# Weight splits ahead of the other work in an expert stage, with four split and eleven raw buffers

## The chip, the cores and the metric

The kernel runs on one core of a Trainium2 chip. The metric is the device time of one execution in microseconds (us), and the median of several executions is compared. The engines of the core are TensorE (PE: matmuls and transposes), VectorE (DVE), ScalarE (ACT), GpSimd (POOL: here gathers, scatters and three subtractions) and SyncE (SP: it issues the weight fetches). Every engine works through its own instructions strictly in order.

## The reference, cut to what matters

One layer: a token mixer (a long convolution beside a gated recurrence), then a mixture of experts in which each expert chooses its tokens. Everything is float32, D is 1024, there are 1024 tokens and 16 experts, and each expert takes its 128 best tokens. The change touches the experts alone:

```python
gates, idx = lax.top_k(jnp.swapaxes(aff, 1, 2), cap)      # cap = 128 tokens for each of 16 experts
xg = jax.vmap(lambda hb, ib: hb[ib])(h, idx)
a = jnp.einsum('becd,edf->becf', xg, w1)                  # 1024 -> 2048
b = jnp.einsum('becd,edf->becf', xg, w3)
y = jnp.einsum('becf,efd->becd', jax.nn.silu(a) * b, w2)  # 2048 -> 1024
y = y * gates[..., None].astype(y.dtype)
# zeros((N, D)).at[idx].add(y), then x + g2 * that, then a last rmsnorm
```

The three weight arrays hold 16 x 3 x 1024 x 2048 float32 numbers, 402 MB, and each is read once.

## The kernel before

Up to about 1010 us the kernel computes the mixer and the routing. Then the expert stage runs to about 2150 us, and a short tail writes the result.

**Pieces.** The weights come in 384 pieces (NP) of 128 x 2048 float32, 1 MB each, 24 to an expert. `fetch(n)` (L988 to L1005) issues piece n on SP into a `raw` buffer; there are NA + NB = 8 + 5 = 13 of these, in two pools. TensorE multiplies in a rounded float32, so `split(n)` makes two parts of a piece: ScalarE casts it (`ehi`, L1219), VectorE subtracts the cast from the piece (`elo`, L1225; GpSimd does it for the first three, L1223). There are NHI = 3 buffers of each part. `mm3` (L63 to L66) adds three products, hi with hi (L64), hi of the tokens with lo of the weights (L65) and lo with hi (L66); a piece takes 12 matmuls of 512 columns. A cast can begin once TensorE has finished the piece three before; a raw buffer is free once the subtraction has read it, and then SP can issue the fetch of the piece 13 further on.

**Steps.** The loop over i at L1265 has 33 steps; steps 2e and 2e + 1 are the halves of expert e's 2048 columns (fc is 0, then 1). A step takes four pieces of w1 (PSUM banks `pa`), a silu by ScalarE (`sa`, two instructions, L1282), four pieces of w3, a multiplication by VectorE (two, L1284), and then four pieces of w2 for the step before (banks `pb`). `take()` (L1245) is called once for a piece: it makes the split of the piece NHI - 1 further on, issues a fetch, and hands out the parts.

**Other work between the pieces.** After each step eight transposes flip `sa` (L1318), ScalarE casts them (`hh`, two, L1320) and VectorE subtracts (two, L1321). After step 2e come the one-hot matrix of expert e + 2's tokens (VectorE, `oh`, L1184), 16 small matmuls that make their row numbers (L1188), a cast (`idx`, L1190) and an indirect gather on GpSimd (L1193); then `transposed(e + 1)`: eight transposes of that expert's tokens (L1203), eight scaled copies by ScalarE (`hf`, L1209), two casts (`hcT`, L1210) and two subtractions by VectorE (L1211). After step 2e + 2 VectorE scales the result of expert e (two, `xg`, L1307) and GpSimd adds its rows to `xacc` in memory (L1312). Below, the pieces of an expert are numbered 0 to 23 by n modulo 24: its first step's w1 is piece 20 to 23 of the expert before, its w3 is 0 to 3, the next step's w1 is 8 to 11 and its w3 12 to 15, and the w2 pieces are 4 to 7 and 16 to 19.

**What sets the order.** The program is written without waits. A scheduler puts the instructions of each engine into one fixed list when the kernel is built, by its own estimate of when each would be ready and by the order in which they were written; the waits follow from the buffers. `after(ins)` (L1024) asks that what is issued inside it stands behind `ins`.

At the start of the stage three pieces are split (their casts run early, at 985 us, beside the routing), two gathers are issued, nine matmuls of the identity with itself are run with no use of the result (L1261), and the first expert's tokens are transposed.

Of the kernel before, what the change touches and what calls it, by code (L numbers as in the profile page):

```python
# [11 lines left out]
F32 = mybir.dt.float32  # L12
# [10 lines left out]
P = 128  # L23
# [4 lines left out]
NE = 16  # L28
# [29 lines left out]
def kernel(ctx: ExitStack, tc: tile.TileContext, T: dict, out: bass.AP, dbg=None, stop=None):  # L58
# [919 lines left out]
    NA, NB, NHI = 8, 5, 3  # L978
# [200 lines left out]
    found = [None]  # L1179

    def gather(e):

        oh = ep.tile([P, 8, P], BF16, name="oh", bufs=1)
        V.tensor_tensor(oh, iot[:].unsqueeze(1).broadcast_to([P, 8, P]), posT[:, :, e:e + 1].broadcast_to([P, 8, P]), ALU.is_equal)  # L1184
        pi = bank("pt", 2)
# [4 lines left out]
        f_ = V.tensor_copy(idx, pi[:, 0:1])  # L1190
        found[0] = found[0] or f_
        xg = ep.tile([P, D + NE], F32, name="xg", bufs=3)
        G.indirect_dma_start(xg[:], None, h2d[:], bass.IndirectOffsetOnAxis(ap=idx[:, 0:1], axis=0))  # L1193
        return idx, xg

    def transposed(e, xg):
        xT = [a[:, :, e % 2 * P:(e % 2 + 1) * P] for a in hcT]
        for b in range(2):
            pt = bank("pt", 2)
            hf = ep.tile([P, 4, P], F32, name="hf", bufs=2)  # L1200
            for c in range(4):
                k = 4 * b + c
                PE.transpose(pt[:, c * P:(c + 1) * P], xg[:, k * P:(k + 1) * P], ident)  # L1203
            for c in range(4):
                k = 4 * b + c
                if e == 0 and b == 1:
                    V.tensor_scalar(hf[:, c, :], pt[:, c * P:(c + 1) * P], gs2[:, k:k + 1], mod2[:, k, 0:1], ALU.mult, ALU.add)
                else:
                    S.activation(hf[:, c, :], pt[:, c * P:(c + 1) * P], AF.Identity, scale=gs2[:, k:k + 1], bias=mod2[:, k, 0:1])  # L1209
            S.copy(xT[0][:, 4 * b:4 * b + 4, :], hf)  # L1210
            V.tensor_tensor(xT[1][:, 4 * b:4 * b + 4, :], hf, f32(xT[0][:, 4 * b:4 * b + 4, :]), ALU.subtract)  # L1211
        return xT

    def split(n):
        if n < NP:
            raw = raws.pop(n)
            hi = eb.tile([P, 2048], F32R, name="ehi", bufs=NHI)
            with after(tl[7]["row"]):
                S.copy(hi, raw)  # L1219
            lo = eb.tile([P, 2048], F32R, name="elo", bufs=NHI)  # L1220
            if n < NHI:
                with after(pieces[-1]):
                    pieces.append(G.tensor_tensor(lo, raw, f32(hi[:]), ALU.subtract))  # L1223
            else:
                V.tensor_tensor(lo, raw, f32(hi[:]), ALU.subtract)  # L1225
            parts[n] = [t.rearrange("p (a b) -> p a b", b=1024) for t in (hi, lo)]
# [16 lines left out]
    at = 0  # L1243

    def take():  # L1245
        nonlocal at
        if at > 0:
            split(at + NHI - 1)
            fetch(at + NHI - 1 + NA + NB)
        at += 1  # L1250
        return parts.pop(at - 1)

    for n in range(NHI):
        split(n)
        fetch(n + NA + NB)
    g = {0: gather(0)}
    g[1] = gather(1)
# [4 lines left out]
    xTs = {0: transposed(0, g[0][1])}  # L1262
    py = None
    hs_ = {}
    for i in range(NS + 1):  # L1265
# [5 lines left out]
        if i < NS:  # L1271
            sa = ep.tile([P, 2, 512], F32, name="sa")
            for nm in range(2):
                pab = [bank("pa", 4) for _ in range(2)]
                for k in range(8):
                    if k % 2 == 0:
                        w = take()
                    for h in range(2):
                        mm3(pab[h], [a[:, k, :] for a in xTs[e]], [a[:, k % 2, h * 512:(h + 1) * 512] for a in w], k == 0, k == 7)
                for h in range(2):  # L1280
                    if nm == 0:
                        silu = S.activation(sa[:, h, :], pab[h], AF.Silu)  # L1282
                    else:
                        V.tensor_tensor(sa[:, h, :], sa[:, h, :], pab[h], ALU.mult)  # L1284
            if i == NS - 1:
                with after(silu):
                    S.activation(idf, ones[:, 0:1], AF.Abs_reciprocal_sqrt)
        if i > 0:
            pe, pf = divmod(i - 1, 2)
            hh = hs_.pop(i - 1)  # L1290
            if pf == 0:
                py = [bank("pb", 2) for _ in range(2)]
            for c in range(8):
                if c % 2 == 0:
                    w = take()
                for h in range(2):
                    mm3(py[h], [a[:, c, :] for a in hh], [a[:, c % 2, h * 512:(h + 1) * 512] for a in w],
                        pf == 0 and c == 0, pf == 1 and c == 7)
# [4 lines left out]
            if pf == 1:  # L1303
                idx, xg = g.pop(pe)
                for h in range(2):
                    hs = slice(h * 512, (h + 1) * 512)
                    V.scalar_tensor_tensor(xg[:, hs], py[h], xg[:, D + pe:D + pe + 1], g2r[:, hs], ALU.mult, ALU.mult)  # L1307
                    if pe == NE - 1:
                        S.copy(yh[0][:, hs], xg[:, hs])
                        V.tensor_tensor(yh[1][:, hs], xg[:, hs], f32(yh[0][:, hs]), ALU.subtract)  # L1310
                if pe < NE - 1:
                    G.indirect_dma_start(xacc[:], bass.IndirectOffsetOnAxis(ap=idx[:, 0:1], axis=0), xg[:, 0:D], None, compute_op=ALU.add)  # L1312
        if i < NS:
            hh = [ep.tile([P, 8, P], F32R, name=f"hh{i_}") for i_ in range(2)]
            for b in range(2):
                pt = bank("pt", 2)
                for c in range(4):
                    PE.transpose(pt[:, c * P:(c + 1) * P], sa[:, b, c * P:(c + 1) * P], ident)  # L1318
                pv = pt.rearrange("p (c t) -> p c t", t=P)
                S.copy(hh[0][:, 4 * b:4 * b + 4, :], pv)  # L1320
                V.tensor_tensor(hh[1][:, 4 * b:4 * b + 4, :], pv, f32(hh[0][:, 4 * b:4 * b + 4, :]), ALU.subtract)  # L1321
            hs_[i] = hh
            if fc == 0:
                if e + 2 < NE:
                    g[e + 2] = gather(e + 2)
                if e + 1 < NE:
                    xTs[e + 1] = transposed(e + 1, g[e + 1][1])
# [152 lines left out]
```

## Time and profile before

| what | value |
|---|---|
| median of 3 runs | 2182.51 us (2178.77 to 2185.27) |
| the profiled execution's own time | 2179.6 us |
| its span in the trace | 2177.8 us |
| mean granted TensorE clock, as a share of full | 0.982 |
| TensorE matmuls busy | 2042.1 us (94%) |
| VectorE busy | 1732.7 us (80%) |
| ScalarE busy | 1243.4 us (57%) |
| bytes moved | 565.95 MB, mean 260 GB/s |

The shares are means over the whole span. The expert stage is a little over half of it, and the other half works with other limits, so what the change is worth has to be read from rows of the stage itself. Matmuls are pipelined: in the timeline each shows about 0.39 us though the next starts 0.23 us later.

### The profile page before, as it was taken

Reading aid. Unit: us, or ns where it says so; the run is one execution under the profiler, and the core shown is the slowest. Engines: PE = TensorE matmul, PEld = TensorE weight load, DVE = VectorE, ACT = ScalarE, POOL = GpSimd, SP = SyncE. Lnnn points to the kernel's source line nnn. Section 1 sums busy time; section 2 is a strip of 40 time slices with the busy share of each in tenths; the row PEclk is TensorE's granted clock in tenths of the full one; section 3 lists DMA queues with packets and bytes.
Section 4 is the critical chain, followed back from the end, with each engine's and each line's share of the span. In section 5 each row is a group of like instructions: output and inputs, shape, how many; then the busy total and the mean of one; then the engine's idle time right before and its main releaser. Section 6 shows DMA issues by size and latency. Waiting matters only on the chain.

```text
span 2177.8 us, 30396 instructions
## 1 busy us (share of the span) xinstructions
PE 2042.1 (94%) x11761; PEld 1613.6 (74%) x11761; DVE 1732.7 (80%) x2051; ACT 1243.4 (57%) x1463; POOL 204.7 (9%) x241
## 2 busy tenths in 40 slices
PE   7997899899999989994999999999999999999997
PEld 2444788798788867773888888787877878787775
DVE  6678357747878877666999999888988889888887
ACT  3566235444432211242777787777777777777774
POOL 1122100100000011124000000000010011000000
PEclk9999899999999999996999999999999999999999
DMA  7875421320243447376999999999999999999992
GB/s 244 267 261 158 150 73 45 117 83 24 62 137 120 131 141 240 109 256 240 359 375 374 393 392 373 354 377 378 382 361 358 389 381 364 361 381 372 362 335 116
DMA packets 185404, 565.95 MB, mean 260 GB/s; under 512 B 15544, under 2 KB 26379, under 8 KB 185260
## 3 DMA queue, kind: packets, MB, share of 16 engines
q1 hardware_dynamic: 147044, 478.41, 59.1%
q0 software_dynamic: 28784, 76.46, 11.6%
q10 hardware_dynamic: 9432, 9.15, 1.3%
q8 instruction: 93, 1.52, 0.3%
q14 instruction: 51, 0.42, 0.1%
HBM read 522.59 MB, written 41.50 MB: 259 GB/s over the span
## 4 chain that ended last, share of the span: by engine, by line
PE 75%; DVE 9%; DMA 6%; issue 6%; ACT 3%; POOL 1%; DVEq 0%; SPq 0%; ACTq 0%; POOLq 0%
PE pa L65 15%; PE pa L66 15%; PE pa L64 14%; PE pb L66 5%; PE pb L65 5%; PE pb L64 5%; DVE elo L1225 2%; PE pb L849 2%; PE pt L866 2%; PE pf L546 2%; ACT ehi L1219 2%; DMA oraw<-in_w_out 1%; PE pt L1318 1%; DVE arena L731 1%; DVE arena L729 1%
## 5 line engine op out<-in xcount | busy, mean ns | idle before, releaser
L1225 DVE TENSOR_TENSOR elo<-raw,ehi 128x2048 fp32r<-128x2048 f32 x381 | 863.1, 2289 | 102.4 <-ACT ehi L1219 98.3
L1219 ACT CAST ehi<-raw 128x2048 fp32r<-128x2048 f32 x384 | 732.9, 1917 | 214.0 <-PE pb L66 94.6
L65 PE MATMUL pa<-elo,hcT 128*128 128x512 f32 x1024 | 406.8, 397 | 14.9 <-DVE elo L1225 14.6
L66 PE MATMUL pa<-ehi,hcT 128*128 128x512 f32 x1024 | 401.0, 392 | 0.0
L64 PE MATMUL pa<-ehi,hcT 128*128 128x512 f32 x1024 | 376.8, 392 | 2.0 <-ACT hcT L1210 1.4
L65 PEld LDWEIGHTS pa<-elo,hcT 128*128 128x128 f32 x1024 | 192.6, 188 | 72.9 <-DVE elo L1225 35.0
L64 PEld LDWEIGHTS pa<-ehi,hcT 128*128 128x128 f32 x1024 | 192.6, 188 | 42.5 <-ACT hcT L1210 1.8
L66 PEld LDWEIGHTS pa<-ehi,hcT 128*128 128x128 f32 x1024 | 192.8, 188 | 37.3
L65 PE MATMUL pb<-elo,hh 128*128 128x512 f32 x512 | 204.9, 400 | 0.0
L66 PE MATMUL pb<-ehi,hh 128*128 128x512 f32 x512 | 200.0, 391 | 0.4 <-DVE hh L1321 0.4
L64 PE MATMUL pb<-ehi,hh 128*128 128x512 f32 x512 | 184.6, 390 | 0.5 <-ACT hh L1320 0.5
L66 PE MATMUL pa<-hT,wlo 128*128 128x512 f32 x448 | 178.8, 400 | 0.3 <-DVE wlo L580 0.3
L64 PE MATMUL pa<-hT,whi 128*128 128x512 f32 x448 | 178.5, 398 | 0.0
L65 PE MATMUL pa<-hT,whi 128*128 128x512 f32 x448 | 176.4, 394 | 0.0
L1312 POOL DMA_INDIRECT xacc<-xg,idx x15 | 45.3, 3022 | 842.5 <-DVE xg L1307 842.5
L64 PEld LDWEIGHTS pb<-ehi,hh 128*128 128x128 f32 x512 | 96.1, 188 | 21.6 <-ACT hh L1320 0.9
L65 PEld LDWEIGHTS pb<-elo,hh 128*128 128x128 f32 x512 | 96.2, 188 | 21.4
L66 PEld LDWEIGHTS pb<-ehi,hh 128*128 128x128 f32 x512 | 96.2, 188 | 18.8 <-DVE hh L1321 0.9
L66 PEld LDWEIGHTS pa<-hT,wlo 128*128 128x128 f32 x448 | 84.4, 188 | 18.7 <-DVE wlo L580 1.2
L64 PEld LDWEIGHTS pa<-hT,whi 128*128 128x128 f32 x448 | 84.5, 189 | 17.0 <-issue 0.5
L65 PEld LDWEIGHTS pa<-hT,whi 128*128 128x128 f32 x448 | 84.5, 189 | 17.0 <-issue 0.2
L546 PE MATMUL pf<-Yh,mt 128*128 128x256 f32 x256 | 74.5, 424 | 17.6 <-ACT he L552 6.2
(407 smaller groups left out, 3099.3 us busy)
## 6 DMA issues: line engine op xcount, KB each, us to landing
raw<-in_exp_w SPq DMA_DIRECT2D x371, 1024.0 KB, 8.0
aw<-in_ada_w SPq DMA_DIRECT2D x96, 256.0 KB, 4.9
wraw<-in_w_in SPq DMA_DIRECT2D x64, 256.0 KB, 3.3
raw<-in_exp_w POOLq DMA_DIRECT2D x13, 1024.0 KB, 8.7
mt<-in_fwm POOLq DMA_DIRECT2D x64, 128.0 KB, 3.4
Hd<-he ACTq DMA_DIRECT2D x32, 256.0 KB, 3.0
wod<-arena POOLq DMA_DIRECT2D x32, 256.0 KB, 3.4
arena<-in_fwm SPq DMA_DIRECT2D x32, 256.0 KB, 3.9
```

Of the source, the lines that this page charges most:

```text
L64: PE.matmul(ps, lhs[0], rhs[0], start=first, stop=False)
L65: PE.matmul(ps, lhs[0], rhs[1], start=False, stop=False)
L66: PE.matmul(ps, lhs[1], rhs[0], start=False, stop=last)
L546: PE.matmul(pt[:, :HC], mt[:, i, :], Y[:, 2 * n + i, :], start=(i == 0), stop=(i == 1))
L729: V.tensor_tensor(kv, kv, view(F2, h, [[2 * h, nb], [LT - h, 2], [0, h]]), ALU.mult)
L731: V.tensor_tensor(qv, qv, view(F2, LT + h, [[2 * h, nq], [-(LT + h), 2], [0, h]]), ALU.mult)
L849: PE.matmul(px[:, j, :], fm[:, j, i, :], Y[:, 2 * n + i, :], start=(i == 0), stop=(i == 1))
L866: PE.matmul(pz[:, j, :], im[:, i, j, :], pp[:, i, :], start=(i == 0), stop=(i == 1))
L1219: S.copy(hi, raw)
L1225: V.tensor_tensor(lo, raw, f32(hi[:]), ALU.subtract)
L1312: G.indirect_dma_start(xacc[:], bass.IndirectOffsetOnAxis(ap=idx[:, 0:1], axis=0), xg[:, 0:D], None, compute_op=ALU.add)
L1318: PE.transpose(pt[:, c * P:(c + 1) * P], sa[:, b, c * P:(c + 1) * P], ident)
```

## The change

Four things are altered, all in the expert stage.

1. **Buffers**: NB goes from 5 to 3 and NHI from 3 to 4, so there are 11 raw buffers, and 4 for each part. `take` becomes `piece`, which splits the piece three further on instead of two and then runs the jobs that are queued. At the start a fourth piece is split, by VectorE, and a fourth fetch issued.
2. **Order on ScalarE and VectorE**: `act()` and `dve()` put the other work (silu, multiplication, `hh`, `hf`, `hcT`, scale, one-hot) behind the cast or the subtraction of the piece three ahead of the one now handed out.
3. **Jobs**: this work is queued with `then` and issued with the next piece, no longer at the end of a step.
4. **Fixed pieces** for the next experts' work: the one-hot after piece 0 and the gather after piece 2 of an expert's first step, and the token transposes in two halves after pieces 1 and 4 of its second step.

The core of the diff:

```diff
-    NA, NB, NHI = 8, 5, 3
+    NA, NB, NHI = 8, 3, 4
...
+    highs, lows = {}, {}
     def split(n):
...
             with after(tl[7]["row"]):
-                S.copy(hi, raw)
+                highs[n] = S.copy(hi, raw)
...
-            if n < NHI:
+            if n < 3:
                 with after(pieces[-1]):
                     pieces.append(G.tensor_tensor(lo, raw, f32(hi[:]), ALU.subtract))
             else:
-                V.tensor_tensor(lo, raw, f32(hi[:]), ALU.subtract)
+                lows[n] = V.tensor_tensor(lo, raw, f32(hi[:]), ALU.subtract)
...
-    def take():
+    jobs = []
+    def piece():
         nonlocal at
         if at > 0:
             split(at + NHI - 1)
             fetch(at + NHI - 1 + NA + NB)
         at += 1
+        while jobs:
+            jobs.pop(0)()
         return parts.pop(at - 1)
+    def act():
+        return after(highs[min(at + NHI - 2, NP - 1)])
+    def dve():
+        return after(lows[min(at + NHI - 2, NP - 1)])
+    def then(f, *a):
+        jobs.append(lambda: f(*a))
+    def gate(sa, pab, i):
+        for h in range(2):
+            with act():
+                r = S.activation(sa[:, h, :], pab[h], AF.Silu)
...
+    def times(sa, pab):
+        for h in range(2):
+            with dve():
+                V.tensor_tensor(sa[:, h, :], sa[:, h, :], pab[h], ALU.mult)
+    def flip_sa(i, sa):
...
+                PE.transpose(pt[:, c * P:(c + 1) * P], sa[:, b, c * P:(c + 1) * P], ident)
+            with act():
+                S.copy(hh[0][:, 4 * b:4 * b + 4, :], pv)
+            with dve():
+                V.tensor_tensor(hh[1][:, 4 * b:4 * b + 4, :], pv, f32(hh[0][:, 4 * b:4 * b + 4, :]), ALU.subtract)
...
+    def mark(e, ohs):
+        with dve():
+            ohs.append(onehot(e))
-    for n in range(NHI):
+    for n in range(3):
         split(n)
         fetch(n + NA + NB)
-    g = {0: gather(0)}
-    g[1] = gather(1)
+    gather(0, onehot(0))
+    gather(1, onehot(1))
...
-    xTs = {0: transposed(0, g[0][1])}
+    for b in range(2):
+        transposed(0, b)
+    for n in range(3, NHI):
+        split(n)
+        fetch(n + NA + NB)
...
+                    if fc == 0 and e + 2 < NE:
+                        if at_ == 0:
+                            then(mark, e + 2, ohs)
+                        if at_ == 2:
+                            then(lambda e_, o: gather(e_, o[0]), e + 2, ohs)
+                    if fc == 1 and e + 1 < NE and at_ in (1, 4):
+                        then(transposed, e + 1, at_ // 4, act, dve)
+                if nm == 0:
+                    then(gate, sa, pab, i)
+                else:
+                    then(times, sa, pab)
...
+            elif pf == 1:
+                then(add_rows, pe, py)
         if i < NS:
...
+            then(flip_sa, i, sa)
```

The names in the rows below: `ehi` and `elo` are the parts of a piece, `sa` the silu and its product, `hh` the flipped `sa`, `hf` and `hcT` the next expert's tokens; the number behind x is how many such instructions follow each other.

VectorE at the start of the stage, before:

```order
L1170 TENSOR_TENSOR pos_8562<-pb,eq 128x128
L1171 TENSOR_TENSOR posT<-pos_8543,pos_8562 128x128
L1184 TENSOR_TENSOR oh<-iot,posT 128x1024
L1190 CAST idx<-pt 128x1
L1184 TENSOR_TENSOR oh<-iot,posT 128x1024
L1190 CAST idx<-pt 128x1
```

and after the change:

```order
L1170 TENSOR_TENSOR pos_8558<-pb,eq 128x128
L1171 TENSOR_TENSOR posT<-pos_8539,pos_8558 128x128
L1232 TENSOR_TENSOR elo<-raw,ehi 128x2048
L1181 TENSOR_TENSOR oh<-iot,posT 128x1024
L1191 CAST idx<-pt 128x1
L1181 TENSOR_TENSOR oh<-iot,posT 128x1024
```

The subtraction of the fourth piece (L1232) now stands between `posT` and the first one-hot, which was L1184 and is L1181.

ScalarE in expert 5 around a silu, before (from the cast of piece 118 on):

```order
L1219 CAST ehi<-raw 128x2048 x3
L1282 ACTIVATE sa<-pa 128x512
L1219 CAST ehi<-raw 128x2048
L1282 ACTIVATE sa<-pa 128x512
L1219 CAST ehi<-raw 128x2048 x8
```

and after (from the cast of piece 120 on):

```order
L1226 CAST ehi<-raw 128x2048 x4
L1277 ACTIVATE sa<-pa 128x512 x2
L1226 CAST ehi<-raw 128x2048 x8
L1295 CAST hh_11522<-pt 128x512 x2
L1226 CAST ehi<-raw 128x2048 x2
```

The two silu instructions (L1282, now L1277) stood with one cast between them, directly behind the cast of piece 120; now both stand together behind that of piece 123.

ScalarE at the token transposes of expert 6 (pieces 129 to 137, so 9 to 17 of expert 5), before, from the two `hh` casts behind the cast of piece 129 on:

```order
L1320 CAST hh_11488<-pt 128x512 x2
L1219 CAST ehi<-raw 128x2048 x2
L1209 ACTIVATE hf<-pt,mod_79,gs_80 128x128 x5
L1210 CAST hcT_88<-hf 128x4x128
L1209 ACTIVATE hf<-pt,mod_79,gs_80 128x128 x3
L1219 CAST ehi<-raw 128x2048
L1210 CAST hcT_88<-hf 128x4x128
L1219 CAST ehi<-raw 128x2048
L1282 ACTIVATE sa<-pa 128x512 x2
L1219 CAST ehi<-raw 128x2048 x8
```

and after, from the two `hh` casts behind the cast of piece 131 on:

```order
L1295 CAST hh_11522<-pt 128x512 x2
L1226 CAST ehi<-raw 128x2048 x2
L1213 ACTIVATE hf<-pt,mod_79,gs_80 128x128 x4
L1226 CAST ehi<-raw 128x2048
L1215 CAST hcT_88<-hf 128x4x128
L1226 CAST ehi<-raw 128x2048
L1277 ACTIVATE sa<-pa 128x512 x2
L1226 CAST ehi<-raw 128x2048
L1213 ACTIVATE hf<-pt,mod_79,gs_80 128x128 x4
L1226 CAST ehi<-raw 128x2048
L1215 CAST hcT_88<-hf 128x4x128
L1226 CAST ehi<-raw 128x2048 x6
```

All eight scaled copies (L1209, now L1213) stood between the casts of pieces 131 and 132; now four stand in front of the cast of piece 134 and four in front of that of 137, and the silu is between them.

TensorE at the same place, before (piece 129):

```order
L66 MATMUL pa<-ehi,hcT_89 128x512
L64 MATMUL pa<-ehi,hcT_88 128x512
L1203 MATMUL pt<-ident,xg 128x128 x8
L65 MATMUL pa<-elo,hcT_88 128x512
L66 MATMUL pa<-ehi,hcT_89 128x512
```

and after (from the end of piece 131 on):

```order
L65 MATMUL pa<-elo,hcT_88 128x512
L66 MATMUL pa<-ehi,hcT_89 128x512
L1206 MATMUL pt<-ident,xg 128x128 x4
L64 MATMUL pa<-ehi,hcT_88 128x512 x2
L1206 MATMUL pt<-ident,xg 128x128 x4
L65 MATMUL pa<-elo,hcT_88 128x512
```

The eight transposes (L1203, now L1206) stood in piece 129; now they stand at the start of piece 132, with two matmuls between the halves.

## Rows read from the trace of the kernel before

**Rows 1.** The page, part 4: share of the chain by engine.

```profile
PE 75%; DVE 9%; DMA 6%; issue 6%; ACT 3%; POOL 1%; DVEq 0%; SPq 0%; ACTq 0%; POOLq 0%
```

**Rows 2.** The page, part 5: operation | busy us, mean ns | idle, releaser.

```profile
L1225 DVE TENSOR_TENSOR elo<-raw,ehi 128x2048 fp32r<-128x2048 f32 x381 | 863.1, 2289 | 102.4 <-ACT ehi L1219 98.3
L1219 ACT CAST ehi<-raw 128x2048 fp32r<-128x2048 f32 x384 | 732.9, 1917 | 214.0 <-PE pb L66 94.6
```

**Rows 3.** Stretches: us, busy by engine, PEclk, DMA share, GB/s; two whole experts.

```profile
1185.65:1254.27 68.62, 68.62 (x330) 56.72 (x329) 62.67 (x40) 53.41 (x43) 2.71 (x2) 1.00 1.01 384
1462.54:1533.13 70.59, 69.62 (x329) 56.33 (x328) 62.85 (x38) 53.05 (x42) 5.31 (x2) 1.00 1.00 375
1200.00:1250.00 50.00, 50.00 (x226) 41.39 (x225) 45.03 (x26) 36.49 (x22) 0.00 (x0) 1.00 1.01 398
```

**Rows 4.** VectorE timeline, scale of an expert: start, us; 12 more between.

```profile
1185.65 1.41 DVE L1307 SCALAR_TENSOR_TENSOR xg<-pb,xg,g2r 128x512 f32<-128x512 f32 x2
...
2099.94 1.43 DVE L1307 SCALAR_TENSOR_TENSOR xg<-pb,xg,g2r 128x512 f32<-128x512 f32 x2 [0.69 <-PE pb L66]
```

**Rows 5.** Waits of TensorE, 1340 to 2040 us: total, times, longest.

```profile
PE pa L65 <- DVE elo L1225: 9.6, 10, 1.0
```

**Rows 6.** TensorE timeline, last expert: rows with a wait [idle before <-releaser].

```profile
2107.02 0.50 PE L65 MATMUL pa<-elo,hcT 128*128 128x512 f32 x1 [0.38 <-DVE elo L1225]
...
2116.43 0.50 PE L65 MATMUL pa<-elo,hcT 128*128 128x512 f32 x1 [0.96 <-DVE elo L1225]
...
2120.39 0.50 PE L65 MATMUL pa<-elo,hcT 128*128 128x512 f32 x1 [0.90 <-DVE elo L1225]
...
2138.01 0.50 PE L64 MATMUL pb<-ehi,hh 128*128 128x512 f32 x1 [0.45 <-ACT hh L1320]
```

**Rows 7.** Timeline of all engines, one stall of TensorE at 1443 us.

```profile
1433.82 1.91 ACT L1219 CAST ehi<-raw 128x2048 fp32r<-128x2048 f32 x1 [0.81 <-PE pa L66]
...
1438.58 0.60 ACT L1282 ACTIVATE sa<-pa 128x512 f32<-128x512 f32 x1 [2.85 <-PE pa L66]
...
1439.08 1.90 ACT L1219 CAST ehi<-raw 128x2048 fp32r<-128x2048 f32 x1
...
1441.01 4.58 DVE L1225 TENSOR_TENSOR elo<-raw,ehi 128x2048 fp32r<-128x2048 f32 x2 [2.95 <-ACT ehi L1219]
...
1443.35 0.50 PE L65 MATMUL pa<-elo,hcT 128*128 128x512 f32 x1 [0.95 <-DVE elo L1225]
```

**Rows 8.** All waits, 1050 to 2100 us: silu on TensorE.

```profile
ACT sa L1282 <- PE pa L66: 31.5, 12, 2.9
```

**Rows 9.** The page, part 6: fetches of a piece, KB each, us to landing.

```profile
raw<-in_exp_w SPq DMA_DIRECT2D x371, 1024.0 KB, 8.0
```

**Rows 10.** Timeline of all engines, start of the expert stage.

```profile
1008.70 3.96 PE L1261 MATMUL pb<-ident 128*128 128x128 f32 x18
...
1009.54 1.23 DVE L1184 TENSOR_TENSOR oh<-iot,posT 128x1024 bf16<-128x1024 bf16 x1
...
1012.50 0.54 PE L1188 MATMUL pt<-tok,oh 128*128 128x1 bf16 x16
...
1013.53 1.77 POOL L1193 DMA_INDIRECT xg<-h2d,idx  x1 [10.50 <-DVE idx L1190]
...
1018.76 1.97 PE L1203 MATMUL pt<-ident,xg 128*128 128x128 f32 x8 [3.78 <-DMA xg<-h2d,idx]
```

**Rows 11.** The gather line L1193: us to landing.

```profile
DMA to landing us min/median/max: 5.2/8.5/14.1
```

**Rows 12.** Timeline of all engines, flips of the next expert at 1468 us.

```profile
1466.08 1.28 DVE L1321 TENSOR_TENSOR hh<-pt,hh 128x512 fp32r<-128x512 f32 x2
...
1467.99 1.03 PE L1203 MATMUL pt<-ident,xg 128*128 128x128 f32 x8
...
1468.63 1.86 ACT L1209 ACTIVATE hf<-pt,mod,gs 128x128 f32<-128x128 f32 x5 [0.79 <-PE pt L1203]
...
1470.36 0.64 ACT L1210 CAST hcT<-hf 128x512 fp32r<-128x512 f32 x1
```

More of the change, by code (lines that the diff above doesn't have):

```diff
@@ L1177, with onehot, gather @@
     ep = ctx.enter_context(tc.tile_pool(name="ep", bufs=1))
-    found = [None]
-    def gather(e):
+    def onehot(e):
         oh = ep.tile([P, 8, P], BF16, name="oh", bufs=1)
         V.tensor_tensor(oh, iot[:].unsqueeze(1).broadcast_to([P, 8, P]), posT[:, :, e:e + 1].broadcast_to([P, 8, P]), ALU.is_equal)
+        return oh
+    def gather(e, oh):
         pi = bank("pt", 2)
@@ L1261 @@
         PE.matmul(idle[:, 0:P], ident, ident, start=True, stop=True)
-    xTs = {0: transposed(0, g[0][1])}
+    for b in range(2):
+        transposed(0, b)
+    for n in range(3, NHI):
+        split(n)
+        fetch(n + NA + NB)
     py = None
@@ L1272 @@
             sa = ep.tile([P, 2, 512], F32, name="sa")
+            ohs = []
+            xT = tokens_of(e)
             for nm in range(2):
                 pab = [bank("pa", 4) for _ in range(2)]
[L1275 to L1287, printed above, removed]
+                for q in range(4):
+                    w = piece()
+                    for k in (2 * q, 2 * q + 1):
+                        for h in range(2):
+                            mm3(pab[h], [a[:, k, :] for a in xT], [a[:, k % 2, h * 512:(h + 1) * 512] for a in w], k == 0, k == 7)
+                    at_ = 4 * nm + q
+                    if fc == 0 and e + 2 < NE:
[7 more added lines that the diff above has]
+                    then(gate, sa, pab, i)
+                else:
+                    then(times, sa, pab)
         if i > 0:
             pe, pf = divmod(i - 1, 2)
+            while i == NS and jobs:
+                jobs.pop(0)()
             hh = hs_.pop(i - 1)
@@ L1292 @@
                 py = [bank("pb", 2) for _ in range(2)]
[L1293 to L1298, printed above, removed]
+            for q in range(4):
+                w = piece()
+                for c in (2 * q, 2 * q + 1):
+                    for h in range(2):
+                        mm3(py[h], [a[:, c, :] for a in hh], [a[:, c % 2, h * 512:(h + 1) * 512] for a in w],
+                            pf == 0 and c == 0, pf == 1 and c == 7)
             if i == NS:
@@ L1302 @@
                     start_sum(t)
[L1303 to L1312, printed above, removed]
-        if i < NS:
[L1314 to L1327, printed above, removed]
+                add_rows(pe, py)
+            elif pf == 1:
+                then(add_rows, pe, py)
+        if i < NS:
+            then(flip_sa, i, sa)
     for t in range(8):
```

55 lines of the change are left out of this document (38 added, 17 removed).

## The prediction

> **What bounds the kernel now.** I read the chain that ended last first: three quarters of it is TensorE [rows 1]. The costliest groups come next: the subtraction that makes `elo` takes 2.29 us and the cast that makes `ehi` 1.92 us [rows 2], and both are shorter than a piece on TensorE (2.71 us, below), so on the mean neither engine is short of time. Then the stretches. An expert from one scale of its result to the next took 68.62 us early in the stage, with TensorE busy in all of it, and 70.59 us later, with all but the same count of matmuls, at a full granted clock both times [rows 3]. So about 2 us an expert are lost to something that is neither work nor clock. From 1185.65 to 2099.94 us there are 13 experts [rows 4], in 914.29 us; at 68.62 they would take 892.06. The loss there is **22.2 us**.
>
> Where it arises the waits of TensorE tell: ten waits for `elo`, 9.6 us in total, the longest 1.0 [rows 5], one for each expert of that window. That is half of the 2 us; the rest I take to be shorter gaps and slower first matmuls around it, since in the loss by periods they are counted anyway. One of these waits, followed back [rows 7]: ScalarE ends a cast at 1435.73, and then stands 2.85 us in a silu that needs the last matmul of its bank. The cast behind it runs at 1439.08, the subtraction at 1441.01 after 2.95 us of idling, and TensorE stands still until 1443.35. The in-order queue is the fault: the silu came too early, and with three split buffers there is no stock to live on. The silu's waits add up to 31.5 us in 12 rows [rows 8]. In the last expert three more such waits cost 0.38, 0.96 and 0.90 us, and each first matmul behind one shows 0.50 us instead of 0.39 [rows 6], so 2.24 + 3 x 0.11 = **2.6 us**; two for `hh` cost 0.45 each.
>
> **A piece on TensorE.** From 68.62 I take 24 transposes of an expert at 1.03 for eight [rows 12] and the 16 matmuls of a gather at 0.54 [rows 10]: 64.99, or 2.71 us for each of 24 pieces.
>
> **The fourth split buffer and the order.** With four buffers the cast of piece n waits for the end of piece n - 4, not n - 3. Cast and subtraction take 1.92 + 2.29 = 4.21 us, and TensorE needs them after three pieces, 8.1 us: 3.9 us of stock, where three buffers leave 5.4 - 4.2 = 1.2. The silu now stands behind the cast of the fourth piece after its bank's last, as the order of ScalarE shows; that cast waits for a buffer that TensorE frees by ending that very last piece, so the silu has nothing left to wait for. It holds up the next cast by its own 1.2 us (two of 0.60 [rows 7]), which the 3.9 covers. The same holds for the multiplication, the one-hot and the scale on VectorE. I therefore take the whole 22.2 + 2.6 us as gain, and 0.7 more for small ones (the `hh` stall and a few of 0.3): **25.5 us**. If the cover were gone, a silu would cost up to the 2.85 us again.
>
> **The tight place that is left.** The new order puts four scaled copies (`hf`) in front of the cast of piece 14 of an expert, and they wait for transposes that stand behind the whole of piece 11 on TensorE. Count from the end of piece 11, with durations of rows 2, 7 and 12. The copies start 0.64 us after the transposes (1468.63 - 1467.99) and take 0.37 each (1.86 for five): to 2.13. Cast 14 to 4.05, `hcT` 0.64 to 4.69, cast 15 to 6.61, two silus to 7.81, cast 16 to 9.73, four copies to 11.22, cast 17 to 13.14, its subtraction to 15.43. TensorE wants it after eight transposes, five pieces and one matmul (0.23): 1.03 + 13.55 + 0.23 = 14.81. So 0.6 us short by full durations. By the times from one start to the next, shorter by about 0.1 an instruction (the silu follows its cast after 1.79, 1439.08 to 1440.87), these ten or so instructions give back up to 1 us and the shortage is none. VectorE enters with room: it idled 2.95 us in the old order [rows 7] for the same work. Bounds 0 and 0.6 us an expert; I take 0.2, nearer the start-to-start end because that is how a full queue runs. For 15 experts: **+3 us**, bounds 0 and 9.
>
> **Start of the stage.** The fourth subtraction stands between `posT` and the first one-hot on VectorE. The one-hot ran from 1009.54 to 1010.77, but the small matmuls behind it started only at 1012.50, since the idle matmuls held TensorE from 1008.70 to 1012.66 [rows 10]. With 2.29 us more the one-hot ends at 1013.06, so the matmuls start about 0.6 us later, not 2.3. Everything after hangs on it: the gather (1013.53), the transposes at 1018.76, the first matmul. The fetch of piece 14 is now issued as that subtraction ends, 2 us ahead of the gather, and the two share the DMA engines. The quickest gather landed in 5.2 us, the median one, with fetches beside it, in 8.5 [rows 11]. Bounds 0 and 3.3 us; I take 1, because the fetch has a head start and most of its 8.0 us [rows 9] lies before the gather's data. **+1.6 us**, bounds 0.6 and 3.9.
>
> **Two raw buffers fewer.** A raw buffer comes free at the end of its subtraction, and the piece in it is cast 13 pieces later: 13 x 2.94 - 4.2 = 34 us after the issue, against 8.0 to landing [rows 9]: 26 us of reserve. With 11 and the faster pace 11 x 2.86 - 4.2 = 27.3, less 8.0: 19 us. It costs nothing as long as the supply holds: one expert moves 384 GB/s x 68.62 us = 26.4 MB, and at 68.6 us asks for the same 384 that the early expert had, while 398 was moved over 50 us [rows 3].
>
> **The rest** has one answer. Flips of `sa`, gathers, scatters and the second table load keep their number and durations; the gather is issued a whole expert ahead of its use, and the scale of expert 14, three pieces later, leaves the last reads of `xacc` some 30 us. The two `hh` waits of the last step stay in about the size they have.
>
> **A rule against it.** The trace shows 384 to 398 GB/s in stretches without a wait for data [rows 3]. The Trainium skill, page "DMA: Bandwidth & Descriptors", section "Where 436 GB/s comes from", says that for transfers from HBM the limit of about 358 GB/s per core binds, not the fabric's 435. By that rule an expert could not take less than 26.4 / 0.358 = 73.7 us, and the change could gain nothing. The rows contradict it, and the sum goes by them; where supply would bind after all stands under (b).
>
> **The sum.** 2179.6 - 25.5 + 3 + 1.6 = 2158.7 us against the profiled execution. That one lies 2.9 below the median of 2182.51; taken from the median it is 2161.6. I forecast **2160 us**.
>
> **Rivals.**
> (a) *The scaled copies become the new wait.* The tight place costs 0.6 to 1.6 us an expert, because the transposes come later than counted (they need a bank that VectorE frees behind the scale and the `hh` subtractions, 1.41 + 1.28 us). For it: ScalarE has hardly a gap in those pieces. Against it: the margin is missed by 0.6 at most above. At 1.2: 2160 - 3 + 18 = 2175; up to 1.6, 2181. 25 in 100 for up to 1.2 (2167 to 2175), 6 for more (same).
> (b) *Supply.* With 11 buffers the reserve of 19 us is eaten and TensorE waits for pieces. Slower than before decides where 15 experts lose the gain of 15 x 2.0 us and the reserve too: (30 + 19) / 15 = 3.3 us above 68.6, which is 71.9 us, so below 26.4 MB / 71.9 = 367 GB/s. A little below that, at 360, an expert takes 73.3: 15 x 4.7 - 19 = 51 lost against 30 gained, about 2203. For it: the DMA engines show a busy share of 1.01 in that early expert. Against it: 384 and 398 with no wait for data, and the 26 us of reserve that the present kernel is counted to have. 5 in 100. The rule above would end here, too.
> (c) *The change doesn't do what it says*, the waits stay with only their place changed: about 2182. The order on ScalarE speaks against it. 2 in 100.
>
> **How the numbers follow.** Forecast as counted (0 to 0.6 us an expert, start 0.6 to 3.9, either base: 2153 to 2167): 62 in 100. With (a) up to 1.2 the chance of faster is 87. About 0.3%, 6.5 us, is what a measurement of this kernel can tell from no change. Same: 6 of (a) and 2 of (c), so 8. Slower: (b), 5. The range runs from 2152 to 2175: it takes in the forecast and most of (a), and leaves out some 15 in 100.
>
> **What would show it.** Right: no wait of TensorE for `elo` over 0.3 us between 1340 and 2040, a period of scales of 68.6 to 68.9 us at 384 GB/s, the silu's wait harmless, and the first matmul of the stage 0.6 to 3.9 us later. (a) is seen as a wait for `elo` once an expert, at the third to sixth piece behind the token transposes, with a row of ScalarE `hf` waiting for `pt` ahead of it. (b) is seen as ScalarE's casts waiting for the DMA of `raw`. The prediction is wrong if the period stays above 70 us, or if the early 68.62 was not the floor.

## The result and the profile after

The changed kernel takes **2156.28 us** (2155.32 to 2157.41) where the kernel before took 2180.64 (2178.73 to 2185.27) beside it: a ratio of 0.988, interval 0.9865 to 0.9896. That is 24.4 us less, inside the predicted range of 2152 to 2175 and 3.7 us under the predicted 2160.

The page of the changed kernel: the chain by engine, then the groups of the subtraction, of the cast and of the matmuls that read `elo` (operation, count | busy us, mean ns | idle before).

```profile
PE 76%; issue 11%; DMA 6%; DVE 5%; ACT 1%; POOL 1%; DVEq 0%; POOLq 0%; ACTq 0%; SPq 0%
...
L1232 DVE TENSOR_TENSOR elo<-raw,ehi 128x2048 fp32r<-128x2048 f32 x381 | 860.0, 2287 | 100.7 <-ACT ehi L1226 95.9
L1226 ACT CAST ehi<-raw 128x2048 fp32r<-128x2048 f32 x384 | 732.1, 1922 | 204.5 <-PE pa L66 129.3
L65 PE MATMUL pa<-elo,hcT 128*128 128x512 f32 x1024 | 402.1, 393 | 0.0
```

And the same group of matmuls on the page of the kernel before:

```profile
L65 PE MATMUL pa<-elo,hcT 128*128 128x512 f32 x1024 | 406.8, 397 | 14.9 <-DVE elo L1225 14.6
```

The two splitting instructions take as long as they did [rows 2]. What is gone is the idle time in front of the matmuls on `elo`: 14.9 us before, 0.0 now. VectorE still idles 100 us for casts, but nobody waits for that any more.

Two whole experts, by the stretch view (us, busy by engine, granted clock, DMA share, GB/s):

```profile
1193.79:1262.39 68.60, 68.60 (x330) 56.82 (x329) 62.62 (x39) 53.16 (x43) 2.93 (x2) 1.00 1.01 385
1468.23:1536.84 68.61, 68.61 (x330) 56.82 (x329) 61.99 (x39) 52.87 (x43) 4.57 (x2) 1.00 1.01 384
```

The early expert of the kernel before took 68.62 us and the late one 70.59 [rows 3]; now both take the former, and TensorE is busy in all of it. VectorE's timeline has the first and the last of the 13 periods of the scale (start, us, what):

```profile
1193.79 1.40 DVE L1305 SCALAR_TENSOR_TENSOR xg<-pb,xg,g2r 128x512 f32<-128x512 f32 x2
...
2084.53 1.40 DVE L1305 SCALAR_TENSOR_TENSOR xg<-pb,xg,g2r 128x512 f32<-128x512 f32 x2
```

That is 890.74 us for what took 914.29 [rows 4], 23.55 less. From the first token transposes to the last scale the stage went from 1130.49 to 1102.39 us, **28.1 less**. The span shrank by 23.6 only: in this execution the work ahead of the stage, which the change doesn't touch, ended 4.2 us later (`posT` at 1013.39, not 1009.21). The way from `posT` to the first transposes is 9.94 us, not 9.55. So -28.1 + 4.2 + 0.4 = -23.5.

Whether those 4.2 us belong to the kernel was asked of the other profiles: `posT` stood at 1011.01 in a second profile of the changed kernel, and between 1007.93 and 1013.53 in nine profiles of other kernels, whatever their buffers and order (one with a subtraction in its way, below, is left aside). It is scatter of the mixer between executions, and it is why small differences below are read from the stage and not from the total.

The stage scatters too, at its start. Ahead of the first token transposes TensorE mostly idles, waiting for the gather, and at these transposes its granted clock was 0.50 (1.2 GHz) in all profiles but one (the last run below). It rose to 1.00 (2.4 GHz) for good 7.2 us behind the transposes in the profile before, 9.6 us in that of the changed kernel, and after 6.3 to 9.5 us in other runs of the new order. From the first transposes to the first scale the new order took 100.2 us where it rose after 6.3, and 101.8 where it rose after 9.6. So differences of up to 1.6 us between two stages may be the clock alone, and the 28.1 us would, by an estimate from these rows, be about 29 with the clock of the profile before.

### The profile page after: what moved, and what is told of

Its sections match the earlier page's. It is cut to its first block, busy times and chain, and to the rows that moved or that the text cites. A ratio compares the mean times of both kernels' runs of the same rounds, so it can differ in the third digit from the quotient of the medians.

```text
span 2154.2 us, 30387 instructions
## 1 busy us (share of the span) xinstructions
PE 2031.1 (94%) x11761; PEld 1621.0 (75%) x11761; DVE 1721.8 (80%) x2051; ACT 1240.6 (58%) x1463; POOL 183.0 (8%) x239
## 4 chain that ended last, share of the span: by engine, by line
PE 76%; issue 11%; DMA 6%; DVE 5%; ACT 1%; POOL 1%; DVEq 0%; POOLq 0%; ACTq 0%; SPq 0%
PE pa L66 15%; PE pa L64 15%; PE pa L65 15%; PE pb L64 5%; PE pb L66 5%; PE pb L65 5%; PE pb L849 2%; PE pf L546 2%; PE pt L866 2%; PE pt L1292 1%; DMA arena<-in_fwm 1%; PE pd L279 1%; DMA arena<-in_ivm 1%; DVE arena L731 1%; DMA oraw<-in_w_out 1%
## 5 line engine op out<-in xcount | busy, mean ns | idle before, releaser
L1232 DVE TENSOR_TENSOR elo<-raw,ehi 128x2048 fp32r<-128x2048 f32 x381 | 860.0, 2287 | 100.7 <-ACT ehi L1226 95.9
L65 PE MATMUL pa<-elo,hcT 128*128 128x512 f32 x1024 | 402.1, 393 | 0.0
L65 PE MATMUL pb<-elo,hh 128*128 128x512 f32 x512 | 199.2, 389 | 0.0
L1310 POOL DMA_INDIRECT xacc<-xg,idx x15 | 23.8, 1588 | 876.9 <-DVE xg L1305 876.9
```

The source lines that it names most:

```text
L65: PE.matmul(ps, lhs[0], rhs[1], start=False, stop=False)
L1232: lows[n] = V.tensor_tensor(lo, raw, f32(hi[:]), ALU.subtract)
```

## The experiments

The theory: TensorE waited because ScalarE, in order, reached work of another kind too early, and the casts behind it came late. The rivals: the fourth split buffer brings the gain; flips and copies have a share of their own; supply is near its end; the start costs more than counted. The medians come from several sessions, in which the kernel before took 2180.64, 2184.94, 2181.22 and 2186.76 us; each ratio below is taken against the kernel before of the same session, and kernels of different sessions are best compared by stage and period. Stage is the time from the first token transposes to the last scale, period that from scale to scale in the middle of the stage, waits what TensorE waited for `elo` or `ehi` from 1340 to 2040 us.

| kernel | median us | stage us | period us | waits us |
|---|---|---|---|---|
| before | 2180.64 | 1130.5 | 70.6 | 10.1 |
| changed | 2156.28 | 1102.4 | 68.6 | 0 |
| changed, once more | 2154.06 | 1102.3 | 68.6 | 0 |
| buffers alone | 2213.43 | 1163.5 | 74.0 (72.9 to 74.5) | 29.2 |
| order alone | 2153.37 | 1102.8 | 68.7 | 0 |
| order alone, once more | 2154.99 | 1103.9 | 68.7 | 0 |
| silu alone | 2165.75 | 1113.2 | 69.3 | 2.2 |
| buffers and silu | 2191.48 | 1136.9 | 71.7 | 19.0 |
| changed, eight raw buffers | 2158.42 | 1100.9 | 68.6 | 0 |
| changed, copies together | 2173.17 | 1118.2 | 70.2 | 12.6 |

### Buffers alone

```diff
-    NA, NB, NHI = 8, 5, 3
+    NA, NB, NHI = 8, 3, 4
-            if n < NHI:
+            if n < 3:
```

> The kernel before with the buffers alone: four split and eleven raw, the old order (one silu still between the casts of pieces 0 and 1 of an expert). Theory A, the order is what counts: the cast of piece 1 still stands behind a silu that waits for the end of the bank, so one wait of TensorE for elo of about 1 us an expert stays, a period of 69.7 to 70.6 us, 2170 to 2180 us. Theory B, the stock of the fourth buffer is what counts: no such wait, a period of 68.6 us, 2155 to 2160 us.

Measured: 2213.43 us, ratio 1.0136 (1.0105 to 1.0166): slower than before, which neither theory had foreseen. ScalarE's timeline in expert 5 shows three places where it stands still (start, us, what, idle before and its releaser):

```profile
1406.85 1.85 ACT L1209 ACTIVATE hf<-pt,mod,gs 128x128 f32<-128x128 f32 x5 [3.23 <-PE pt L1203]
...
1438.18 1.15 ACT L1320 CAST hh<-pt 128x512 fp32r<-128x512 f32 x2 [3.92 <-PE pb L65]
...
1448.97 0.60 ACT L1282 ACTIVATE sa<-pa 128x512 f32<-128x512 f32 x1 [4.23 <-PE pa L66]
```

The same silu stood 2.85 us before [rows 7] and the copies 0.79 [rows 12]. With one buffer more the casts run a piece further ahead of TensorE, so whatever stands at a fixed place between them comes up to a piece too early, and ScalarE waits longer there. But ScalarE's wait is not yet TensorE's. All the waits of TensorE in the same expert are these three:

```profile
1379.29 0.50 PE L65 MATMUL pa<-elo,hcT 128*128 128x512 f32 x1 [0.95 <-DVE elo L1225]
...
1412.11 0.73 PE L64 MATMUL pa<-ehi,hcT 128*128 128x512 f32 x2 [0.50 <-ACT ehi L1219]
...
1414.44 0.50 PE L65 MATMUL pa<-elo,hcT 128*128 128x512 f32 x1 [1.60 <-DVE elo L1225]
```

The first, in piece 1, is the silu's, and it is as long as with three buffers (0.95 [rows 7]): the fourth buffer neither heals nor worsens it. The other two, in piece 12, are new. The edit left the program's order as written, but the scheduler made another list of it: it moved the token transposes from piece 9 to piece 10 on TensorE and left the copies that wait for them in front of the cast of piece 12, and it moved the flips of `sa` from pieces 17 to 19 to pieces 18 to 20. From the transposes (1406.21) copies, cast and subtraction take 8.2 us, to 1414.38, and without a wait TensorE would come to its first matmul on that `elo` after some 5.7 (an estimate: piece 11 started at 1408.70, and 14 matmuls follow at 0.227). The `hh` casts, for which ScalarE waited 3.92 us, make no wait of TensorE.

And in two experts of three the granted clock falls behind the waits of piece 12: it was 0.50 from 1415.30 on for 3.4 us. In the experts with such a fall the period is 74.5, in the others 72.9, so a fall costs about 1.5 us. The stretch view of the two moments (the third number from the end is the granted clock):

```profile
1411.90:1415.20 3.30, 1.49 (x5) 0.97 (x6) 3.11 (x3) 3.30 (x4) 0.61 (x1) 1.00 1.01 402
1415.30:1418.70 3.40, 3.40 (x10) 2.66 (x9) 3.40 (x2) 3.40 (x4) 0.54 (x1) 0.50 0.90 317
```

Theory A's mechanism holds: the silu's wait of about 1 us stays. Its number doesn't, because the list changed with the buffers. So this run shows that the fourth buffer does not bring the gain; what it would cost with the transposes left in piece 9 was not run.

### Order alone

The changed kernel with the buffers of before.

```diff
-    NA, NB, NHI = 8, 3, 4
+    NA, NB, NHI = 8, 5, 3
```

> The changed kernel with the buffers of before: three split and thirteen raw, the new order (each piece of other work now stands behind the cast two ahead instead of three). Theory A, the order is what counts: the silu still finds its bank finished, and the tightest place counted by hand (the subtractions behind the scale and the flips) keeps 0.3 us, so 0 to 0.5 us an expert are lost: 2155 to 2165 us. Theory B, the stock counts: with 1.2 us of stock each group of other work opens a gap, about 2 us an expert, 2175 to 2182 us.

Measured: 2153.37 us, ratio 0.9863 (0.9834 to 0.9891), a little under the range of Theory A. The second time, against a kernel before of its own:

> The new order with three split and thirteen raw buffers again, as the measure for the run with late idle matmuls on the same chip and against the changed kernel (2154 and 2156 us so far): 2150 to 2156 us; period 68.6 to 68.7 us.

2154.99 us, ratio 0.9857 (0.984 to 0.9873), and in a whole expert of that run:

```profile
1533.23:1601.89 68.66, 68.66 (x330) 56.72 (x329) 62.34 (x40) 53.02 (x43) 4.10 (x2) 1.00 1.01 385
```

The order alone has the whole gain, as far as the time can tell: the ranges of the changed kernel's runs, with medians 2156.28 and 2154.06, and of these two overlap. The traces tell a little more. From the first to the fifteenth scale the order alone took 961.0 and 960.9 us in its two profiles, the changed kernel 959.4 and 959.3. So the fourth buffer is worth 1.6 us of the stage, 0.1 us an expert; 0.9 of it lies in two early experts of 69.1 and 69.0 us.

### The silu alone

The kernel before, with its silus queued to the next piece and ordered behind the cast two pieces ahead; nothing else moves on ScalarE.

```diff
+        while jobs:
+            jobs.pop(0)()
         return parts.pop(at - 1)
...
+        for h in range(2):
+            with after(highs[at + NHI - 2]):
+                silu = S.activation(sa[:, h, :], pab[h], AF.Silu)
```

> The kernel before with one thing altered: both silus stand behind the cast two pieces ahead (on ScalarE behind the casts of pieces 2 and 14 of an expert, instead of 0, 1 and 13). Buffers, token transposes, flips and VectorE's list stay as before. If the early silu is the whole cause: no wait of TensorE for elo over 0.3 us, a period of 68.6 to 68.9 us and 2155 to 2162 us. If it is only the 1 us that the wait shows and the other half of the 2 us an expert is due to flips and copies: a period near 69.6 and 2167 to 2171 us. If the wait only moves to the next place: above 2175 us.

Measured: 2165.75 us, ratio 0.9923 (0.9902 to 0.9945), a period of 69.3: just under the middle case. The waits of TensorE's matmuls in this run, from 1340 to 2040 us:

```profile
PE pa L65 <- DVE elo L1227: 1.7, 2, 1.6
PE pa L64 <- ACT ehi L1221: 0.5, 1, 0.5
```

And those of its weight loads, in the same stretch, here and then in the kernel before:

```profile
PEld pa L65 <- DVE elo L1227: 13.6, 40, 2.0
```

```profile
PEld pa L65 <- DVE elo L1225: 24.9, 47, 1.4
```

So moving one kind of instruction removes 1.3 of the 2.0 us an expert: the wait of 1 us and what hung on it. The other 0.7 remains although hardly a matmul waits. It shows in the second view: four weight loads an expert still find `elo` not quite ready, in pieces 9 and 11 to 13. By the distances between starts in one expert, some 13 matmuls come later than the pitch of 0.23 us, most by 0.09, and lose 1.2 us together; in the changed kernel it is five and 0.45, so this is the 0.7. By their places the hits lie where ScalarE or VectorE has other work ahead of the splits: the scale, the copies and the one-hot in pieces 9 to 13, the multiplication in pieces 5, 6 and 17 to 19. Each kind was not moved by itself. The order alone, which moves them all, and the changed kernel have no such row for `elo` between 1340 and 2040 us.

### Buffers and silu

The edit above, with four split and eleven raw buffers.

> The kernel with the buffers alone (four split, eleven raw, 2213 us) with the silus alone moved behind the cast three pieces ahead. Theory F, there the flips are the fault (the scheduler has spread the eight sa transposes over pieces 18 to 20, and ScalarE stands up to 4 us before the hh casts with the next casts queued behind): the hh wait stays, the period stays above 71 us and the time above 2185 us. Theory S, the early silu is the fault here too: no wait of TensorE for elo, a period near 69.3 us, 2160 to 2170 us.

Measured: 2191.48 us, ratio 1.0031 (1.0017 to 1.0045), period 71.7. The numbers are those of Theory F. ScalarE's waits from 1340 to 2040 us still have the other two kinds of early work:

```profile
ACT hh L1329 <- PE pb L65: 73.8, 20, 4.0
...
ACT hf L1209 <- PE pt L1203: 29.0, 9, 3.2
```

But the waits of TensorE in the same stretch are of one kind only:

```profile
PE pa L65 <- DVE elo L1227: 14.3, 9, 1.6
...
PE pa L64 <- ACT ehi L1221: 4.7, 9, 0.5
```

These are nine times the two waits of piece 12 (0.53 and 1.59 in expert 5), behind the token copies, whose transposes stand in piece 10 here too. So the theory has its number right and the wrong culprit: the flips cost ScalarE up to 4.0 us twice an expert and TensorE no wait. Of the 5.4 us an expert that the buffers alone lose against the floor (74.0 less 68.6), 2.3 go with the silu: 1.3 are its wait and what hangs on it (72.9 to 71.7), 1.0 the clock, which hardly falls here (once, before 1340). Of the 3.1 that are left the two waits behind the copies are 2.1, and the slower matmuls around them and the hits of the silu-alone run the rest.

### Eight raw buffers

```diff
-    NA, NB, NHI = 8, 3, 4
+    NA, NB, NHI = 8, 0, 4
```

> The changed kernel with eight raw buffers instead of eleven. If the reserve is what was counted (a buffer comes back 8 x 2.86 - 4.2 = 18.7 us after its fetch is issued, 8.2 to landing), 10 us are left over and the time stays within 2 us of 2156. If the supply were near its end (the rival of the prediction), casts would wait for raw and the time would rise by 5 us or more.

Measured: 2158.42 us, ratio 0.9885 (0.9856 to 0.9915), with a period of 68.61; ScalarE has no wait for `raw` from 1340 to 2040 us. Three more raw buffers could go. A whole expert of this run:

```profile
1194.55:1263.16 68.61, 68.61 (x330) 56.83 (x329) 62.17 (x40) 53.14 (x43) 2.92 (x2) 1.00 0.99 375
```

The total is 2.1 us above the changed kernel's, a little more than expected, and its profile puts that at the start: here the fourth subtraction ran earlier, in the middle of the routing on VectorE and beside GpSimd's three.

```profile
989.29 13.46 POOL L1230 TENSOR_TENSOR elo<-raw,ehi 128x2048 fp32r<-128x2048 f32 x3 [1.19 <-ACT ehi L1226]
...
999.20 5.71 DVE L1232 TENSOR_TENSOR elo<-raw,ehi 128x2048 fp32r<-128x2048 f32 x1
```

It took 5.71 us, not 2.29, and the search for the threshold around it lasted 29.5 us from its first instruction (L1131) to `posT`, not 24.0. The stage was 1.5 shorter, but that is the clock: it rose 6.3 us behind the first transposes, not 9.6, and the 1.5 lies ahead of the first scale.

### The copies together

The changed kernel with both halves of the token transposes queued after piece 1.

```diff
-                    if fc == 1 and e + 1 < NE and at_ in (1, 4):
-                        then(transposed, e + 1, at_ // 4, act, dve)
+                    if fc == 1 and e + 1 < NE and at_ == 1:
+                        for b in range(2):
+                            then(transposed, e + 1, b, act, dve)
```

> The changed kernel with both halves of the token transposes' copies in front of the cast of piece 14 (eight copies and one hcT cast, in the place of four copies). By the count of the tight place: copies and cast end 0.64 + 8 x 0.35 + 0.6 = 4.0 us after the transposes, the cast at 5.9, the subtraction at 8.1, wanted at 6.7: a wait of about 1.4 us for each of 15 experts, a period of 70.0 and 2175 to 2180 us. If the tight place has more room than counted: under 0.5 us an expert, 2156 to 2163 us.

Measured: 2173.17 us, ratio 0.9951 (0.9936 to 0.9966), a little under what was expected, a period of 70.2, ten waits of 1.26 us on the mean. One of them in the timeline: the transposes, the copies, the cast, its subtraction, and TensorE's wait.

```profile
1407.12 0.60 PE L1206 MATMUL pt<-ident,xg 128*128 128x128 f32 x4
...
1407.76 1.86 ACT L1213 ACTIVATE hf<-pt,mod,gs 128x128 f32<-128x128 f32 x5 [3.97 <-PE pt L1206]
...
1411.04 1.94 ACT L1226 CAST ehi<-raw 128x2048 fp32r<-128x2048 f32 x1
...
1413.01 2.29 DVE L1232 TENSOR_TENSOR elo<-raw,ehi 128x2048 fp32r<-128x2048 f32 x1 [2.16 <-ACT ehi L1226]
...
1415.36 0.50 PE L65 MATMUL pa<-elo,hcT 128*128 128x512 f32 x1 [1.27 <-DVE elo L1232]
```

From the transposes the cast starts after 3.92 us and the subtraction ends after 8.18; counted by hand were 4.0 and 8.1. The tight place is where the prediction put it, and the wait is of the size that was counted (1.4). So the distance between the two halves is worth some 16 us of the stage.

### The start of the stage

> The changed kernel again, as the measure for the runs on the start of the stage on the same chip: 2154 to 2159 us. If the 4 us by which its mixer ended later than that of the kernel before belong to single executions and not to the kernel, the one-hot's predecessor on VectorE ends anywhere from 1008 to 1014 us here too.

> The changed kernel with the fourth subtraction ordered behind the second one-hot on VectorE; the scheduler then puts the nine idle matmuls of TensorE behind the two gathers' matmuls. Both covers are gone: the gather's matmuls follow the one-hot at once, 2.1 us earlier after the end of routing (from 3.7 to 1.6 us behind posT), and the first token transposes come 2 us earlier, 9.9 to 7.9 us behind posT: 2 us faster than the changed kernel, 2152 to 2156. If the idle matmuls are needed early for the granted clock, the first matmuls of the stage stay longer at 0.50 and the gain is smaller.

> As the run with the late fourth subtraction, but with the nine idle matmuls kept ahead of the first gather's matmuls, as in the kernel before. Only the subtraction's own price is taken away: the gather's matmuls start when the idle matmuls end, 0.5 us earlier than in the changed kernel (3.2 instead of 3.7 us behind posT), so 0.4 to 0.6 us faster than it, if the count of the prediction (0.6 us, not the whole 2.29) is right; 2.2 us faster if the subtraction was fully exposed.

Both edits order the fourth subtraction behind the second one-hot; the second also writes the order of the idle matmuls down.

```diff
+                with after(marks[1]) if n == 3 else ExitStack():
+                    lows[n] = V.tensor_tensor(lo, raw, f32(hi[:]), ALU.subtract)
```

Measured, on one chip: 2154.06 (2153.17 to 2159.59), 2154.31 (2152.55 to 2157.92) and 2155.17 us (2153.07 to 2158.19). No difference. The first edit was to change the order on TensorE too, and in the trace it did not: the idle matmuls stayed in front, so the two runs are of one kind. In the last run, the idle matmuls and the gather's own:

```profile
1011.36 2.79 PE L1327 MATMUL pb<-ident 128*128 128x128 f32 x18
...
1013.99 0.54 PE L1192 MATMUL pt<-tok,oh 128*128 128x1 bf16 x16
```

The gather's matmuls stood 2.12 us behind `posT` (1011.87) here and 3.18 in the other; in two profiles of the changed kernel it was 3.73 and 3.74, before 3.29. Where the subtraction is out of the way, the end of the idle matmuls decides, and their time varies with the granted clock: 2.79 us at a mean of 0.80 here, 3.85 us at 0.56 in the other. Against the kernel before and the first of these runs the price of the subtraction is 0.4 to 0.6 us, against the quickest idle matmuls 1.6, and the whole 2.29 in none.

A last run put the idle matmuls behind the second gather's, in the order-alone kernel:

> The new order with three split and thirteen raw buffers (2153 us), and the nine idle matmuls of TensorE behind the small matmuls of the second gather instead of ahead of the first. The first gather's matmuls then follow the one-hot at once (1.6 instead of 2.9 us behind posT) and the idle ones run while the gather is in flight: first token transposes 7.1 to 7.8 us behind posT instead of 9.1, so 1.3 to 2 us faster; more if TensorE's granted clock in the first matmuls of the stage is higher, less if it stays at 0.50 longer.

2154.98 us (2154.14 to 2157.49), beside 2154.99 for the same kernel without the edit. The transposes came 8.08 us behind `posT`, where the two profiles without it have 9.10 and 8.38. They began when the gather landed, not when the idle matmuls let go:

```profile
1021.36 0.86 PEld L1208 LDWEIGHTS pt<-ident,xg 128*128 128x128 f32 x8 [0.19 <-DMA xg<-h2d,idx]
```

So what is won is what the gather is issued earlier, 2.71 us behind `posT` and not 3.93 and 3.12. The forecast stood on the slower of the two profiles. What is left is below what the total can show. No kernel here is faster than the changed one by more than the scatter.

## Why the prediction was right, step by step

**The reading of the loss.** Right in size: the 68.62 us of the early expert was the floor, and every expert now stands on it. Where the loss sits was half right. The prediction laid the second half of the 2 us to gaps and slow matmuls around the silu's wait. The silu-alone run shows 0.3 us of it there; 0.7 stays when that wait is gone and belongs to the other early work.

**The order.** The step that says the silu came too early is shown: moved alone it gives 15.5 us. The step that gave the credit to the fourth buffer as well ("with three split buffers there is no stock to live on") failed. With three buffers and the new order TensorE has no wait for a split in the middle of the stage, and the fourth buffer is worth 1.6 us in all. With four and the old program the silu's wait is 0.95 us as before: it hangs on the end of a bank, and the cast and the subtraction come behind it, however many buffers there are. The count of stock, 1.2 us with three and 3.9 with four, was not wrong as arithmetic, but the new order hardly needs the larger one. This failure could not show in the number, since the change has both parts.

**The sum of the gain.** 25.5 us was forecast and 28.1 came, with nothing to take off for the tight place. The 13 periods that the sum puts at 22.2 gave 23.55: 1.2 of the difference is that the last two of them have no gather and take 68.05 and 68.02, not 68.62. Counted on TensorE from the first matmul of one piece to that of another, 24.6 lies between pieces 36 and 372 (14 experts), 0.7 between 12 and 36 (left out of the sum), 3.3 in the last twelve pieces (3.3 in the sum, 2.6 and 0.7), and the first twelve took 0.5 longer, since the clock stayed at 0.50 for 2.4 us more. The sum is not quite of one piece: the 0.7 counts the `hh` stall as gained, and a later sentence lets both `hh` waits stay. Of the two, 0.45 us each, one is gone and one shrank:

```profile
2114.98 0.50 PE L64 MATMUL pb<-ehi,hh 128*128 128x512 f32 x1 [0.24 <-ACT hh L1295]
```

**The tight place.** Taken at 3 us, bounds 0 and 9; measured 0. In the changed kernel, from the transposes to the first matmul that wants the subtraction of piece 17:

```profile
1475.67 0.60 PE L1206 MATMUL pt<-ident,xg 128*128 128x128 f32 x4
...
1476.31 1.51 ACT L1213 ACTIVATE hf<-pt,mod,gs 128x128 f32<-128x128 f32 x4 [3.98 <-PE pt L1206]
...
1484.57 1.54 ACT L1213 ACTIVATE hf<-pt,mod,gs 128x128 f32<-128x128 f32 x4
...
1485.95 1.96 ACT L1226 CAST ehi<-raw 128x2048 fp32r<-128x2048 f32 x1
...
1487.94 2.29 DVE L1232 TENSOR_TENSOR elo<-raw,ehi 128x2048 fp32r<-128x2048 f32 x1 [0.90 <-ACT ehi L1226]
...
1490.68 0.39 PE L65 MATMUL pb<-elo,hh 128*128 128x512 f32 x1
```

The subtraction ends at 1490.23, 14.56 us behind the transposes, and TensorE comes to it at 1490.68. So 0.45 us are left, where full durations said 0.6 short: the chain took 0.9 less than 15.43, and TensorE came 0.2 later than 14.81. Here the chain from one start to the next was the right measure. And (a) had no part in the time.

**The start.** Taken at 1.6, bounds 0.6 and 3.9; measured 0.4, just under the lower bound, so that this sign of being right was missed.

```profile
1012.88 3.67 PE L1325 MATMUL pb<-ident 128*128 128x128 f32 x18
...
1013.60 2.29 DVE L1232 TENSOR_TENSOR elo<-raw,ehi 128x2048 fp32r<-128x2048 f32 x1
1015.80 1.22 DVE L1181 TENSOR_TENSOR oh<-iot,posT 128x1024 bf16<-128x1024 bf16 x1
...
1017.12 0.54 PE L1189 MATMUL pt<-tok,oh 128*128 128x1 bf16 x16 [0.57 <-issue]
...
1018.14 1.77 POOL L1193 DMA_INDIRECT xg<-h2d,idx  x1 [12.51 <-DVE idx L1191]
...
1023.33 1.97 PE L1206 MATMUL pt<-ident,xg 128*128 128x128 f32 x8 [3.72 <-DMA xg<-h2d,idx]
```

The 0.57 us in front of the gather's matmuls is the exposed part of the 2.29; the idle matmuls covered the rest [rows 10]. The mis-sized term is the 1 us for the fetch beside the gather: from its issue to the transposes it took 5.19 us, before 5.23.

**The two raw buffers.** Right, and with room: eight are enough. The rival of supply (b) falls with that run. The rule of the Trainium skill that would have forbidden the gain ("DMA: Bandwidth & Descriptors", "Where 436 GB/s comes from") does not hold for this core, the only one that the program uses: 384 and 385 GB/s flowed for whole experts.

**The sum.** The bounds that go with the main case, 2153 to 2167, do not follow from its terms: these give 2179.6 - 25.5 + 0 + 0.6 = 2154.7 to 2182.5 - 25.5 + 9 + 3.9 = 2169.9. The time lies within either. The terms that were off (gain 2.6 too small, residue 3 and start 1.2 too large) all point one way and make 6.8 us; the mixer's 4.2 us in the profiled execution went against them. The steps were too cautious by more than the 3.7 us by which the forecast missed, so that the forecast came as near as it did is in part luck.

## What to carry to other kernels

Where engines work in order, look for work that waits in front of the instructions that feed the bottleneck, and move it behind the one whose own wait covers it; this costs nothing and was the whole gain here. Don't add buffers without reading the new order of every engine: here the scheduler listed one group of transposes a piece later and left the work that waits for it in its place, and a loss of 2 us an expert became one of 5.4. Go by the waits of the engine that bounds the kernel: ScalarE's waits of 4 us at the flips cost TensorE none. A chain in a full queue is better counted from start to start than by full durations.

## What was not expected of the hardware

In one profile a subtraction of 128 x 2048 on VectorE took 5.71 us beside GpSimd's, and 2.29 by itself. Matmuls around an operand that was ready only just in time started about 0.09 us late even where no wait of their own is shown; these hits made the last 0.7 us an expert. The same nine idle matmuls took from 2.76 us, at a mean granted clock of 0.81, to 4.15 us, at 0.52, in different executions. Two waits of 0.5 and 1.6 us on TensorE within one piece were followed, in two experts of three, by a fall of the granted clock to 0.50 for 3.4 us. And one core drew 384 to 398 GB/s from memory for tens of microseconds with nobody waiting for data.
